# Eight start addresses for the MLP operands of a two-layer decoder trunk, and other cuts at both ends of the program

## The chip, the cores and the metric

One core of a Trainium2 chip runs the whole program. The metric is the device time of one execution in microseconds (us), from the start of the program to its end.

## What is computed

The input has 256 tokens of width 1024 in float32. Two layers are run. Each is an attention with 16 heads of width 64, then an MLP of inner width 4096; after each of the two stands a residual and a layer norm. Cut to what matters:

```python
h = x
for i in range(DEPTH):                       # 2
    ln1_g, ln1_b, w1, w2, ln2_g, ln2_b = channel[i]
    h = layer_norm(DEEPNORM_ALPHA * h + mixers[i % N_MIXERS](h), ln1_g, ln1_b)
    h = layer_norm(DEEPNORM_ALPHA * h + squared_relu_mlp(h, w1, w2), ln2_g, ln2_b)

def squared_relu_mlp(x, w1, w2):
    return jnp.square(jax.nn.relu(x @ w1)) @ w2
```

The mixer of layer 0 is stick-breaking attention, that of layer 1 a softmax attention with rotary positions (with 256 tokens there is one block, so it is plainly causal).

## The kernel before

Every product with a weight matrix is made as three matmuls in the type fp32r: an operand a is split in a high part (ScalarE, a cast) and a low part (VectorE, a minus its high part), and hi\*hi + hi\*lo + lo\*hi is summed in PSUM. The helper `mm3` (line 192) issues the three, `split` (line 201) the cast and the subtraction.

**Weights.** All weight matrices are cut on the host in units of 512x512, 1 MB each. A unit is loaded by SyncE's queue into one of three `raw` buffers and split into `hi` and `lo`, from a pool of five pairs (`Unit`, lines 239 to 263). The first two units are loaded and split in four slices, so that TensorE can begin early; so is the transposed input `xt` (lines 300 to 313).

**Stages of a layer.** The projections of attention run with attention's own work between them (lines 557 to 583), then the output projection `wo` (lines 585 to 611) and the first layer norm, then the MLP in eight chunks c of 512 inner columns each (lines 677 to 701). In chunks 0 and 1 `up_tok` takes x as the stationary operand and streams 512 columns of weights; in chunks 2 to 7 `up` takes weights as stationary and streams 256 columns of x. `down` takes the inner values (`hh`, `hl`) as stationary and streams 512 columns of weights. Per chunk, `up` has 96 matmuls of 256 columns, `up_tok` 48 of 512 columns and `down` 48 of 512 columns. The last two `down` chunks are done token half by token half (t = 0, then t = 1), and each token half is followed by its layer norm (`norm`, line 350) and, in layer 1, by its output (`to_out`, line 388).

**Order.** `Plan` (line 64) sets the order of the instructions on each engine at build time from costs written in the kernel; TensorE's own order is as the code is written, and the other engines' work is drawn in by time and rank.

**Addresses.** Tiles lie one behind another in each partition's memory. `shift(GAP[0])` and `shift(GAP[1])` (lines 217 and 222) put 224 and 288 unused bytes ahead of and behind x, h and v. In the built program the high and low parts of x begin at 96 modulo 128 bytes, those of all weights at 32, those of the inner values (and of attention's output) at 96. Buffers of `t2k` (line 180) are 2080 bytes apart, so the values `r`, which `up_tok` transposes, begin at 0, 32, 64 or 96, by the buffer.

Of the kernel before, what the change touches and what calls it, by code (L numbers as in the profile page):

```python
# [7 lines left out]
F32 = mybir.dt.float32  # L8
# [21 lines left out]
GAP = (224, 288)  # L30
# [124 lines left out]
def trunk(ctx: ExitStack, tc: tile.TileContext, x, xt, cst, cstb, w, ln, out):  # L155
# [12 lines left out]
    small = pool("small", 12)  # L168
# [49 lines left out]
    xh = one.tile([P, KT, T], F32R, tag="xh", name="xh")  # L218
    xl = one.tile([P, KT, T], F32R, tag="xl", name="xl")
# [19 lines left out]
    class Unit:  # L239
        def __init__(self, i):  # L240
# [34 lines left out]
    warm = one.tile([P, 512], BF16, tag="warm", name="warm")  # L275
# [17 lines left out]
    masks = one.tile([P, 2 * DEPTH + 1, P], BF16, tag="masks", name="masks")  # L293
# [56 lines left out]
    def norm(t, banks, ready, gb, after, base):  # L350
        g, b, got = gb
        sm = small.tile([P, 16], F32, tag="sm", name="sm")
        halves = [slice(n * 512, n * 512 + 512) for n in range(2)]
        last = []
        for n, s in enumerate(halves):
            y = dve(512, lambda n=n, s=s: nc.vector.scalar_tensor_tensor(
                h[t][:, s], h[t][:, s], ALPHA, banks[n], op0=ALU.mult, op1=ALU.add),
                after=[ready[n], base], rank=0, give=[("acc", 1)])
            last.append(dve(512, lambda n=n, s=s: nc.vector.bn_stats(sm[:, 6 * n:6 * n + 6], h[t][:, s]), after=[y], rank=0))
        ag = dve(10, lambda: nc.vector.bn_aggr(sm[:, 12:14], sm[:, 0:12]), after=last, rank=0)  # L360
        ep = dve(10, lambda: nc.vector.tensor_scalar(sm[:, 14:15], sm[:, 13:14], LN_EPS, None, op0=ALU.add), after=[ag], rank=0)
# [425 lines left out]
```

## Time and profile before

| | |
|---|---|
| median of 2 runs | 605.96 us (605.09 to 606.82) |
| the profiled execution | 606.12 us |
| its span, first to last instruction | 604.4 us, mean granted TensorE clock 0.993 |
| TensorE matmuls busy | 592.5 us, 98% of the span |
| VectorE, ScalarE busy | 389.5 us (64%), 290.7 us (48%) |
| read from HBM | 107.7 MB, 180 GB/s over the span |

The span lacks 1.7 us of the execution's time. Busy time of TensorE is no pace: matmuls are pipelined, and one shows a duration of some 276 ns (256 columns) though the next starts after about 114 ns. The pace is read from the starts, or from stretches of the chain that hold matmuls alone, by their count.

### The profile page before, as it was taken

The numbers are of one execution on the slowest core, as the hardware profiler recorded it, in microseconds if no ns is written. First come the engines' busy times: TensorE is split into PE (matmuls) and PEld (weight loads), VectorE is DVE, ScalarE is ACT, GpSimd is POOL, SyncE is SP. The second block draws the span as 40 slices with busy tenths as digits, with TensorE's granted clock in tenths as the row PEclk, the third lists the DMA queues.
The fourth block names the chain that finished last, engine by engine and source line by source line (L and its number), as shares of the span: only waits on it lengthen the run. The fifth ranks groups of instructions, "written<-read, shape, count | busy, mean of one in ns | idle before, by whom it ended". The sixth has DMA issues, their size and how long they took to land.

```text
span 604.4 us, 8761 instructions
## 1 busy us (share of the span) xinstructions
PE 592.5 (98%) x3640; PEld 508.3 (84%) x3640; DVE 389.5 (64%) x489; ACT 290.7 (48%) x419; POOL 24.6 (4%) x30
## 2 busy tenths in 40 slices
PE   7999999999999999999999999999999999999994
PEld 6899987878899899898877777778798998898883
DVE  5687774787546445555789777758676537537444
ACT  5676663436435444543535654635356426435410
POOL 0000000000000000000032022001000000000000
PEclk8999999999999999999999999999999999999998
DMA  8984337075565456447165334442764374365201
GB/s 280 367 332 157 110 140 269 21 262 184 201 239 210 154 195 250 157 150 278 65 219 205 140 140 139 140 140 78 270 230 187 140 279 150 153 255 190 90 0 69
DMA packets 17751, 109.31 MB, mean 181 GB/s; under 512 B 1968, under 2 KB 2352, under 8 KB 5680
## 3 DMA queue, kind: packets, MB, share of 16 engines
q1 hardware_dynamic: 17712, 108.76, 48.6%
q8 instruction: 28, 0.46, 0.3%
q14 instruction: 11, 0.09, 0.0%
HBM read 107.71 MB, written 1.05 MB: 180 GB/s over the span
## 4 chain that ended last, share of the span: by engine, by line
PE 95%; DVE 2%; DMA 1%; ACT 1%; SPq 0%; issue 0%; DVEq 0%; ACTq 0%
PE dn_ps L190 29%; PE up_ps L190 28%; PE wo_ps L190 7%; PE qkT_ps L190 7%; PE v_ps L190 7%; PE qk_ps L190 7%; PE sc L190 3%; PE o L502 2%; PE xt L379 1%; DMA raw<-in_wqkv 1%; PE tp L549 1%; DVE lo L205 1%; DVE xl L205 1%; PE ht_ps L656 1%; PE pt_ps L484 1%; PE pt_ps L486 1%
## 5 line engine op out<-in xcount | busy, mean ns | idle before, releaser
L205 DVE TENSOR_TENSOR lo<-raw,hi 128x1024 fp32r<-128x1024 f32 (+1 forms) x196 | 229.7, 1213 | 47.4 <-ACT hi L204 45.7
L204 ACT CAST hi<-raw 128x1024 fp32r<-128x1024 f32 (+1 forms) x196 | 192.0, 1033 | 62.4 <-issue 42.4
L190 PE MATMUL up_ps<-xh,hi 128*128 128x256 f32 x384 | 106.3, 277 | 0.0
L190 PE MATMUL up_ps<-xl,hi 128*128 128x256 f32 x384 | 106.1, 276 | 0.0
L190 PE MATMUL up_ps<-xh,lo 128*128 128x256 f32 x384 | 106.1, 276 | 0.0
L190 PE MATMUL dn_ps<-hi,hl 128*128 128x512 f32 x256 | 100.9, 394 | 0.0
L190 PE MATMUL dn_ps<-lo,hh 128*128 128x512 f32 x256 | 100.4, 392 | 0.0
L190 PE MATMUL dn_ps<-hi,hh 128*128 128x512 f32 x256 | 99.5, 389 | 0.0
L190 PEld LDWEIGHTS up_ps<-xl,hi 128*128 128x128 f32 x384 | 72.1, 188 | 0.5
L190 PEld LDWEIGHTS up_ps<-xh,hi 128*128 128x128 f32 x384 | 72.1, 188 | 0.5
L623 DVE SCALAR_TENSOR_TENSOR r<-up_ps,r 128x512 f32<-128x512 f32 x32 | 22.0, 688 | 77.9 <-ACT r L621 77.9
L190 PEld LDWEIGHTS up_ps<-xh,lo 128*128 128x128 f32 x384 | 72.1, 188 | 0.0
L621 ACT ACTIVATE r<-up_ps 128x512 f32<-128x512 f32 x32 | 19.1, 596 | 94.8 <-PE up_ps L190 94.8
L190 PEld LDWEIGHTS dn_ps<-lo,hh 128*128 128x128 f32 x256 | 48.1, 188 | 10.6
L190 PEld LDWEIGHTS dn_ps<-hi,hh 128*128 128x128 f32 x256 | 48.1, 188 | 10.2
L190 PEld LDWEIGHTS dn_ps<-hi,hl 128*128 128x128 f32 x256 | 48.1, 188 | 9.6
L190 PE MATMUL qkT_ps<-xh,hi 128*128 128x256 f32 x128 | 37.7, 295 | 1.7 <-ACT hi L204 1.7
L190 PE MATMUL qkT_ps<-xh,lo 128*128 128x256 f32 x128 | 36.6, 286 | 0.2 <-DVE lo L205 0.2
L190 PE MATMUL qkT_ps<-xl,hi 128*128 128x256 f32 x128 | 36.3, 284 | 0.0
L204 ACT CAST xh<-xt 128x512 fp32r<-128x512 f32 x12 | 7.0, 587 | 42.9 <-PE xt L379 41.1
L190 PEld LDWEIGHTS qkT_ps<-xh,hi 128*128 128x128 f32 x128 | 24.9, 195 | 2.8 <-ACT hi L204 2.4
L190 PE MATMUL v_ps<-hi,xh 128*128 128x512 f32 x64 | 26.4, 413 | 0.0
(97 smaller groups left out, 888.8 us busy)
## 6 DMA issues: line engine op xcount, KB each, us to landing
raw<-in_w SPq DMA_DIRECT2D x64, 1024.0 KB, 5.0
raw<-in_wqkv SPq DMA_DIRECT2D x22, 1024.0 KB, 5.1
raw<-in_wo SPq DMA_DIRECT2D x8, 1024.0 KB, 4.8
raw<-in_wqkv SPq DMA_DIRECT2D x8, 256.0 KB, 6.1
gb<-in_l_ln_g SPq DMA_DIRECT2D x4, 512.0 KB, 3.6
gb<-in_l_ln_b SPq DMA_DIRECT2D x4, 512.0 KB, 5.0
h<-in_x SPq DMA_DIRECT2D x2, 512.0 KB, 8.1
out<-h SPq DMA_DIRECT2D x4, 256.0 KB, 2.1
```

What stands on the lines that cost most here:

```text
L190: nc.tensor.matmul(ps, sta, mov, start=start, stop=stop)
L204: f = lambda: nc.scalar.copy(hi(), src())
L205: g = lambda: nc.vector.tensor_tensor(lo(), src(), hi().bitcast(F32), op=ALU.subtract)
L379: nc.tensor.transpose(XB[t][:, n, k * P:(k + 1) * P], h[t][:, (4 * n + k) * P:(4 * n + k + 1) * P], ident)
L484: nc.tensor.transpose(ps[:, j, 0:P], pj[:, T:T + P], ident)
L486: nc.tensor.transpose(ps[:, j, T:T + P], pj[:, P:T], ident)
L502: nc.tensor.matmul(o[HD * j:HD * j + HD, 0, kt * P:T], v[kt][:, hd * HD:(hd + 1) * HD], pt[:, 0:T] if kt == 0 else pt[:, T:T + P], start=k ...
L549: nc.tensor.transpose(tb["tp"][:, pr, c0:c0 + P], QK[g, t]["qk"][:, e * T + pr * P:e * T + pr * P + P], ident)
L621: nc.scalar.activation(box["r", n], ps, AF.Relu)
L623: return dve(512, lambda: nc.vector.scalar_tensor_tensor(box["r", n], ps, 0.0, box["r", n], op0=ALU.max, op1=ALU.mult), after=[a], rank=0. ...
L656: nc.tensor.transpose(box["ht"][:, 0, k * P:(k + 1) * P], box["r", 0][:, k * P:(k + 1) * P], ident)
```

## The change

It has three parts.

1. **Places.** Tiles of weight parts and of inner values get 128 bytes more, and the values begin at an offset in them (`apart`, `pair`, `place`). All other operands stay at the places modulo 128 that they have before (weights 32, x 96, inner values and attention's output 96). In the MLPs the places go by chunk c, with PLACE[c] = 32, 0, 16, 48, 64, 80, 96, 112 for c = 0 to 7. Layer 0: both weights of chunk c at PLACE[c], x and inner values at 96. Layer 1: the first weight of chunk c at PLACE[c] and x at 112 (from the first layer norm on); the second weight at 32 and the inner values of chunk c at PLACE[c] + 64 modulo 128, that is 96, 64, 80, 112, 0, 16, 32, 48.
2. **Start.** The slices of x, and those of the first two weight units, are stored on the host one behind another, so that each load reads one contiguous piece; before, each partition's rows of a slice lay 8 KB apart. The tile of zeros for the first matmuls (`warm`) shares its memory with the masks.
3. **End.** In layer 1, for the last token half, the second 512 output columns of the last chunk are made as two halves of 256, each followed by its residual and its statistics; the last scaling and the last output of these columns are cut in halves, too. The statistics' small tiles come from a pool of their own.

```diff
-GAP = (224, 288)
+GAP = (128, 96)
+PLACE = (32, 0, 16, 48, 64, 80, 96, 112)
...
+    xs_hl = [one.tile([P, KT * T + 32], F32R, tag=f"x{s}", name=f"x{s}") for s in "hl"]
+    x_at = [96]
+
+    def xpart(s, k, q):
+        o = x_at[0] // 4
+        return xs_hl[s][:, o:o + KT * T].rearrange("p (k q) -> p k q", k=KT)[:, k, q]
...
+    def apart(pool, n, at, tag, name, k):
+        y = pool.tile([P, n + 32], F32R, tag=tag, name=name)
+        return y[:, at // 4:at // 4 + n].rearrange("p (k q) -> p k q", k=k)
+
+    def place(name, j):
+        if name == "w10" or name == "w20" or name == "w11":
+            return PLACE[j // 2]
+        return 32
+
+    def pair(name, at):
+        return [apart(st, 4 * T, (at + 64) % 128, "s" + s, name + s, 4) for s in "hl"]
...
-                    nc.sync.dma_start(self.raw[:, k0:k1, :], w[name][j][:, k0:k1, :])
+                    nc.sync.dma_start(self.raw[:, k0:k1, :], w["first"][i, k0] if i < 2 else w[name][j])
...
-                            self.hi = splits.tile([P, 4, 512], F32R, tag="hi", name=f"hi{i}")
-                            self.lo = splits.tile([P, 4, 512], F32R, tag="lo", name=f"lo{i}")
+                            self.hi, self.lo = [apart(splits, 2048, place(name, j), s, f"{s}{i}", 4) for s in ("hi", "lo")]
...
-                xs[ks.start // 4][:, ks.start % 4:(ks.stop - 1) % 4 + 1, :], xt[:, ks, :]), rank=3 + 0.01 * (k // 4) + 0.001 * (k % 4) - 0.0005)
+                xs[ks.start // 4][:, ks.start % 4:(ks.stop - 1) % 4 + 1, :], xt[ks.start]), rank=3 + 0.01 * (k // 4) + 0.001 * (k % 4) - 0.0005)
...
+        parts = [(n, c0, c1, tk) for n in range(2) for c0, c1, tk in ready[n]]
+        for i, (n, c0, c1, tk) in enumerate(parts):
+            s = slice(512 * n + c0, 512 * n + c1)
+            y = dve(c1 - c0, lambda n=n, s=s, c0=c0, c1=c1: nc.vector.scalar_tensor_tensor(
+                h[t][:, s], h[t][:, s], ALPHA, banks[n][:, c0:c1], op0=ALU.mult, op1=ALU.add),
+                after=[tk, base], rank=0, give=[("acc", 1)] if c1 == 512 else ())
+            last.append(dve(c1 - c0, lambda i=i, s=s: nc.vector.bn_stats(sm[:, 6 * i:6 * i + 6], h[t][:, s]), after=[y], rank=0))
...
+            fine = [(0, 256), (256, 512)] if len(ready[n]) > 1 else [(0, 512)]
+            for c0, c1 in fine:
+                s = slice(512 * n + c0, 512 * n + c1)
+                end.append(dve(c1 - c0, lambda s=s: nc.vector.scalar_tensor_tensor(
+                    h[t][:, s], h[t][:, s], rs, b[:, s], op0=ALU.mult, op1=ALU.add), after=[pw, cen[n]], rank=0))
+                after(t, n, end[-1], s)
...
+        if l:
+            x_at[0] = 112
...
-                HT[c] = (st.tile([P, 4, T], F32R, tag="sh", name="hh"), st.tile([P, 4, T], F32R, tag="sl", name="hl"))
+                HT[c] = pair("h", (PLACE[c] + 64) % 128 if l else 96)
...
+                loop = [(n, k, c0, c1) for n, c0, c1 in ((0, 0, 512), (1, 0, 256), (1, 256, 512)) for k in range(4)]
...
+        if l == 0:
+            give("first", units[:2].transpose(0, 2, 1, 3))
```

(The pool that `pair` takes from begins at 64 modulo 128, so that the argument of `pair` is the place itself. The places named here are those of the built program.)

Apart from the end, no engine's order changes. On VectorE, the end of the program before (the layer norm of the last token half; `h_91` is its residual stream):

```order
L356 SCALAR_TENSOR_TENSOR h_91<-h_91,dn_ps 128x512
L359 BN_STATS sm<-h_91 128x6
L356 SCALAR_TENSOR_TENSOR h_91<-h_91,dn_ps 128x512
L359 BN_STATS sm<-h_91 128x6
L360 BN_AGGR sm<-sm 128x2
L361 TENSOR_SCALAR sm<-sm 128x1
L363 SCALAR_TENSOR_TENSOR h_91<-h_91,sm,gb_3824 128x512 x2
L367 SCALAR_TENSOR_TENSOR h_91<-h_91,sm,gb_3825 128x512 x2
```

And of the change, the same place (`h_94` is the same tile):

```order
L384 SCALAR_TENSOR_TENSOR h_94<-h_94,dn_ps 128x512
L387 BN_STATS sm<-h_94 128x6
L384 SCALAR_TENSOR_TENSOR h_94<-h_94,dn_ps 128x256
L387 BN_STATS sm<-h_94 128x6
L384 SCALAR_TENSOR_TENSOR h_94<-h_94,dn_ps 128x256
L387 BN_STATS sm<-h_94 128x6
L388 BN_AGGR sm<-sm 128x2
L389 TENSOR_SCALAR sm<-sm 128x1
L392 SCALAR_TENSOR_TENSOR h_94<-h_94,sm,gb_3826 128x512 x2
L399 SCALAR_TENSOR_TENSOR h_94<-h_94,sm,gb_3827 128x512
L399 SCALAR_TENSOR_TENSOR h_94<-h_94,sm,gb_3827 128x256 x2
```

The second pair of residual and statistics became two pairs of half the width, and the last of the two scalings two of half the width; SyncE's last output is cut likewise, and TensorE's last 12 matmuls of 512 columns became 24 of 256.

On SyncE's queue, the first loads before:

```order
L304 DMA h_90<-in_xt 128x256
L248 DMA raw_114<-in_wqkv 128x512
L304 DMA h_90<-in_xt 128x256
L248 DMA raw_114<-in_wqkv 128x512
L304 DMA h_90<-in_xt 128x512
L248 DMA raw_114<-in_wqkv 128x512 x2
L304 DMA h_91<-in_xt 128x512
```

And of the change:

```order
L329 DMA h_93<-in_xt 128x256
L274 DMA raw_116<-in_first 128x512
L329 DMA h_93<-in_xt 128x256
L274 DMA raw_116<-in_first 128x512
L329 DMA h_93<-in_xt 128x512
L274 DMA raw_116<-in_first 128x512 x2
L329 DMA h_94<-in_xt 128x512
```

Order and sizes are the same; the weight slices come from the array `first`, and the slices of x from an array each.

## Rows read from the trace of the kernel before

**Rows 1.** The page: busy time of each engine, share of the span and instructions.
```profile
PE 592.5 (98%) x3640; PEld 508.3 (84%) x3640; DVE 389.5 (64%) x489; ACT 290.7 (48%) x419; POOL 24.6 (4%) x30
```
**Rows 2.** Chain that ended last: start us, us, what, and count of its instructions.
```profile
68.24 3.54 PE qkT_ps L190 x30
75.15 4.10 PE qkT_ps L190 x36
...
167.62 10.91 PE up_ps L190 x96
178.53 10.98 PE dn_ps L190 x48
...
530.84 10.91 PE up_ps L190 x96
541.75 10.98 PE dn_ps L190 x48
```
**Rows 3.** Stretches of one `up` chunk: busy us of each engine, clock, DMA share, GB/s.
```profile
core 0: us, PE busy (x) PEld busy (x) DVE busy (x) ACT busy (x) POOL busy (x), PEclk, DMA share, GB/s
168.50:169.86 1.36, 1.36 (x14) 1.36 (x13) 1.36 (x2) 1.36 (x2) 0.00 (x0) 1.00 0.92 367
177.01:178.37 1.36, 1.36 (x15) 1.36 (x13) 0.00 (x0) 0.00 (x0) 0.00 (x0) 1.00 0.13 48
```
**Rows 4.** Timeline of TensorE in these stretches: start us, duration us, what.
```profile
168.39 0.28 PE L190 MATMUL up_ps<-xh,lo 128*128 128x256 f32 x1
...
169.07 0.28 PE L190 MATMUL up_ps<-xh,lo 128*128 128x256 f32 x1
...
177.12 0.28 PE L190 MATMUL up_ps<-xl,hi 128*128 128x256 f32 x1
...
177.69 0.28 PE L190 MATMUL up_ps<-xh,hi 128*128 128x256 f32 x1
```
**Rows 5.** Chain: the four transposes that follow each of the first `up_tok`.
```profile
132.85 0.44 PE ht_ps L656 x4
...
136.75 0.44 PE ht_ps L656 x4
...
142.01 0.44 PE ht_ps L656 x4
...
147.69 0.44 PE ht_ps L656 x4
```
**Rows 6.** The stretch at the lower clock, and starts of matmuls in it.
```profile
11.80:15.20 3.40, 3.40 (x19) 3.40 (x18) 3.36 (x6) 2.53 (x5) 0.00 (x0) 0.50 1.05 426
...
12.19 0.42 PE L190 MATMUL qkT_ps<-xh,lo 128*128 128x256 f32 x1
...
13.26 0.41 PE L190 MATMUL qkT_ps<-xl,hi 128*128 128x256 f32 x1
```
**Rows 7.** The page: weight loads of `up`; busy us, mean ns of one, idle before.
```profile
L190 PEld LDWEIGHTS up_ps<-xl,hi 128*128 128x128 f32 x384 | 72.1, 188 | 0.5
```
**Rows 8.** The start: TensorE's wait, who ended it, and DMA in two stretches.
```profile
7.80 0.28 PE L190 MATMUL qkT_ps<-xh,lo 128*128 128x256 f32 x1
9.78 0.38 PE L190 MATMUL qkT_ps<-xh,hi 128*128 128x256 f32 x1 [1.71 <-ACT hi L204]
...
8.22 0.71 ACT L309 CAST xh<-h 128x256 fp32r<-128x256 f32 x2 [2.34 <-DMA h<-in_xt]
9.11 1.29 ACT L204 CAST hi<-raw 128x512 fp32r<-128x512 f32 x2 [0.18 <-DMA raw<-in_wqkv]
...
5.00:9.00 4.00, 3.08 (x24) 2.68 (x23) 1.53 (x5) 1.33 (x3) 0.00 (x0) 1.00 0.89 208
9.00:12.70 3.70, 2.69 (x17) 2.49 (x18) 3.36 (x8) 3.37 (x7) 0.00 (x0) 0.87 1.08 416
```
**Rows 9.** Timeline: the end of the program, and an operation of VectorE of half the width.
```profile
596.20 0.40 PE L190 MATMUL dn_ps<-hi,hl 128*128 128x512 f32 x1
596.64 0.69 DVE L356 SCALAR_TENSOR_TENSOR h<-h,dn_ps 128x512 f32<-128x512 f32 x1 [1.33 <-PE dn_ps L190]
597.36 0.69 DVE L359 BATCH_NORM_STATS2 sm<-h 128x6 f32<-128x512 f32 x1
...
599.72 1.41 DVE L367 SCALAR_TENSOR_TENSOR h<-h,sm,gb 128x512 f32<-128x512 f32 x2
...
8.66 0.76 DVE L310 TENSOR_TENSOR xl<-h,xh 128x256 fp32r<-128x256 f32 x2 [2.05 <-ACT xh L309]
```
**Rows 10.** The page: the output's DMA issues, KB each, median us to landing.
```profile
out<-h SPq DMA_DIRECT2D x4, 256.0 KB, 2.1
```

More of the change, by code (lines that the diff above doesn't have):

```diff
@@ L273, in retire @@
         plan.give([("split", n)], clock["pe"])
-    warm = one.tile([P, 512], BF16, tag="warm", name="warm")
+    masks = one.tile([P, 2 * DEPTH + 1, P], BF16, tag="masks", name="masks")
+    warm = masks[:, 0:4, :].rearrange("p a b -> p (a b)")
     nc.gpsimd.memset(warm, 0.0)
@@ L351, in norm @@
         g, b, got = gb
-        sm = small.tile([P, 16], F32, tag="sm", name="sm")
-        halves = [slice(n * 512, n * 512 + 512) for n in range(2)]
+        sm = small.tile([P, 24], F32, tag="sm", name="sm")
+        mv, ve, rs = sm[:, 18:20], sm[:, 20:21], sm[:, 21:22]
         last = []
[L355 to L359, printed above, removed]
@@ L363, in norm @@
+        ag = dve(10, lambda: nc.vector.bn_aggr(mv, sm[:, 0:6 * len(parts)]), after=last, rank=0)
+        ep = dve(10, lambda: nc.vector.tensor_scalar(ve, mv[:, 1:2], LN_EPS, None, op0=ALU.add), after=[ag], rank=0)
+        pw = plan.op("pool", 1.0, lambda: nc.gpsimd.tensor_tensor(rs, ve, nhalf, op=ALU.pow), after=[ep], rank=0)
+        cuts = [slice(n * 512, n * 512 + 512) for n in range(2)]
         cen = [dve(512, lambda s=s: nc.vector.scalar_tensor_tensor(
-            h[t][:, s], h[t][:, s], sm[:, 12:13], g[:, s], op0=ALU.subtract, op1=ALU.mult), after=[ag, got], rank=0) for s in halves]
+            h[t][:, s], h[t][:, s], mv[:, 0:1], g[:, s], op0=ALU.subtract, op1=ALU.mult), after=[ag, got], rank=0) for s in cuts]
@@ L365, in norm @@
         end = []
-        for n, s in enumerate(halves):
-            end.append(dve(512, lambda s=s: nc.vector.scalar_tensor_tensor(
-                h[t][:, s], h[t][:, s], sm[:, 15:16], b[:, s], op0=ALU.mult, op1=ALU.add), after=[pw, cen[n]], rank=0))
-            after(t, n, end[-1])
+        for n in range(2):
+            fine = [(0, 256), (256, 512)] if len(ready[n]) > 1 else [(0, 512)]
[4 more added lines that the diff above has]
+                after(t, n, end[-1], s)
@@ L370, in norm, with to_x @@
         return end
     XB = {}
-    def to_x(t, n, done):
+    def to_x(t, n, done, _):
         def turn():
@@ L386, in trunk, with to_out @@
     XTP = [None] * NT
-    def to_out(t, n, done):
-        s = slice(n * 512, n * 512 + 512)
+    def to_out(t, n, done, s):
         plan.op("sp", 0.75, lambda: nc.sync.dma_start(out[tok(t), s], h[t][:, s]), after=[done], rank=0)
@@ L664, in down @@
             last = c == NFC - 1
-            ready = [None, None]
-            for n, k in [(n, k) for n in range(2) for k in range(4)] if last else [(n, k) for k in range(4) for n in range(2)]:
+            ready = [[], []]
+            if not last:
+                loop = [(n, k, 0, 512) for k in range(4) for n in range(2)]
+            elif l < DEPTH - 1 or t == 0:
+                loop = [(n, k, 0, 512) for n in range(2) for k in range(4)]
+            else:
+                loop = [(n, k, c0, c1) for n, c0, c1 in ((0, 0, 512), (1, 0, 256), (1, 256, 512)) for k in range(4)]
+            for n, k, c0, c1 in loop:
                 plan.wait([us[n].tok[k], HR[c][t][k]])
                 hh, hl = HT[c]
-                mm3(dn[t][n], hh[:, k, tok(t)], hl[:, k, tok(t)], us[n].hi[:, k, :], us[n].lo[:, k, :],
-                    c == 0 and k == 0, last and k == 3)
-                ready[n] = here()
+                mm3(dn[t][n][:, c0:c1], hh[:, k, tok(t)], hl[:, k, tok(t)], us[n].hi[:, k, c0:c1], us[n].lo[:, k, c0:c1],
+                    c == 0 and k == 0, last and k == 3 and c1 == 512)
+                if k == 3:
+                    ready[n].append((c0, c1, here()))
             if t == 1:
@@ L762 @@
     give("x", x)
-    give("xt", x.reshape(T, KT, P).transpose(2, 1, 0))
+    xt = x.reshape(T, KT, P).transpose(2, 1, 0)
+    pieces = {}
+    for k, n in X_LOADS.items():
+        give(f"xt{k}", xt[:, k:k + n, :])
+        pieces[k] = aps[f"xt{k}"]
     cst, cstb = _constants()
```

27 lines of the change are left out of this document (15 added, 12 removed).

## Prediction

> **What bounds the kernel now.** I read the page first: TensorE is busy for 98% of the span, VectorE for 64%, ScalarE for 48% [rows 1]. So the kernel is TensorE's time, and the change can matter in two ways: by the pace at which matmuls follow each other, or by the few microseconds at both ends in which TensorE waits or is done. The busy share says nothing of the pace, so I read the chain of waits next: in the MLPs it is runs of matmuls with nothing between them. An `up` chunk is 96 matmuls of 256 columns in 10.91 us, 113.6 ns each; a `down` chunk is 48 of 512 columns in 10.98 us, 228.8 ns each; in layer 1 the same figures stand [rows 2]. The reader is to see how even that is: the pace is a property of the matmul, not of what runs beside it. It shows again in two stretches of one chunk. In the first, VectorE and ScalarE are busy throughout and DMA moves 367 GB/s; in the second both are idle and DMA moves 48 GB/s [rows 3]. Six matmuls start within 0.68 us (113 ns each) in the one, five within 0.57 us (114 ns) in the other [rows 4].
>
> **The floor.** In the one stretch where the clock is at 0.50, the level of 1.2 GHz, matmuls of 256 columns start 1.07 us apart by five, 214 ns each [rows 6]: 256 columns at 1.2 GHz are 213.3 ns, so nothing is lost there. At 2.4 GHz the same would be 106.7 ns, and 213.3 ns for 512 columns. The MLPs lose 7 ns of each 256-column matmul and 15.5 ns of each 512-column one. That loss is all that better places could win.
>
> **Places.** 1152 matmuls of 256 columns (6 chunks x 96 x 2 layers) and 816 of 512 columns get a new place for an operand (`up_tok` 48 + 96, `down` 7 chunks x 48 in each layer; chunk 0 keeps its places apart from x in layer 1). They take 1152 x 0.1136 + 816 x 0.2288 = 131 + 187 = 318 us, 53% of the span. No row shows these matmuls at other places, so I bound the cost from both sides.
> - Lowest: the whole loss goes, 1152 x 7.0 ns + 816 x 15.5 ns = 8.1 + 12.6 = 20.7 us.
> - Highest that a row of the same matmul shows: in layer 0's attention, runs of the same form are either at 114 ns (36 in 4.10 us) or at 118 ns (30 in 3.54 us), both at the places 32 and 96 [rows 2]. If all 1152 fell to 118 ns, they would cost 1152 x 4.4 = 5.1 us. That two levels stand at one pair of places also says that place alone does not set the pace.
> - Nearest row for the place itself: the transposes after `up_tok` read `r` from buffers that begin at 0, 96, 64 and 32 modulo 128, in this order, with the other operand always at 32. Four take 0.44 us each time [rows 5]. They move a column only every 0.86 ns, so they could hide a small stall; but they are the only matmuls here whose places differ.
>
> I take zero, since it is what that nearest row shows, and since memory traffic of other engines leaves the pace alone [rows 3, 4]. The casts, subtractions and DMAs that write to the new places lie on engines with slack [rows 1]; should one grow by a tenth, VectorE would still be below 72%.
>
> The Trainium skill ("SBUF — State Buffer", section on the two separate sides) says that TensorE has ports of its own and never waits on anyone, with a second, independent read port for weight loads. By that rule the places change nothing at all, and the sum is that of the two ends alone; the equal pace beside busy and idle engines [rows 3, 4] agrees as far as other engines go, while no run here shows the two read ports against each other.
>
> **Start.** TensorE waits from about 7.9 us (0.11 us after its start at 7.80) to 9.78, 1.9 us. The wait's chain: the cast of the first weight unit's third slice starts at 9.11 when its DMA lands, and the slice of x ahead of it had landed only at 8.2 [rows 8]. From 5 to 9 us the DMA moves 208 GB/s, after 9 us 416 GB/s [rows 8]. Contiguous slices could speed up the first stretch. If they took the wait away, the stretch at the lower clock that follows it would go, too: about 16 matmuls at 214 instead of 114 ns, 1.6 us [rows 6]. The most is 1.9 + 1.6 = 3.5 us. Against it: after 9 us the queue still carries slices with the same 8 KB stride (x and the second unit), at full speed [rows 8]. So the stride is not plainly the cause, and I count a quarter, 0.9 us; the bounds are 0 and 3.5. What is saved is kept: TensorE is the bound behind it. The masks' DMA now has to wait for the warm matmuls, which are over 5 us before it is issued.
>
> **End.** After the last matmul (start 596.20) residual and statistics take 0.69 us each on VectorE [rows 9]. At 256 columns an operation of VectorE takes 0.38 us (0.76 for two) [rows 9], so the two save 2 x 0.31 = 0.6 us; the first half's pair lies beside the second half's matmuls (12 x 113.6 = 1.36 us for 0.76 us of work). The 24 matmuls of 256 columns take 24 x 113.6 = 2.73 us in place of 12 x 228.8 = 2.75 us. Cutting the last scaling adds one operation's fixed cost: 0.70 + 2 x 0.38 against 1.41 us, +0.05. The last output is 128 KB in place of 256; of its 2.1 us [rows 10] I take off 0.25 us, half of what 256 KB take at some 400 GB/s, with 0 as the other bound. Together -0.8 us (-0.5 to -1.0).
>
> **Sum.** The profiled execution took 606.12 us, 1.7 us more than its span, and 0.2 us more than the median of 605.96. 606.12 - 0.9 - 0.8 + 0 = 604.4 us. Two per cent, 12.1 us, is about what a measurement of this kernel can tell from no change.
>
> **Rivals.**
> 1. *The places move the loss* (faster). With half of the 20.7 us gone the time is 594.1 us, with all of it 583.8. For: the loss is there at 2.4 GHz and not at 1.2 [rows 2, 6], so something that reads memory cannot quite follow, and 16 bytes might matter to it. Against: the places go through all eight, so a good one serves an eighth of the chunks, and the new ones would have to be nearly all better. By over 2% only if more than half of the loss goes.
> 2. *Operands at one place collide* (slower). The next weights are loaded while the present columns stream; a load takes 188 ns [rows 7] and hides only because loads overlap matmuls and each other. If both reads met when their operands begin at the same place, the load would come out of hiding and a 256-column matmul would last 188 instead of 113.6 ns, +74 ns; at 512 columns it stays covered by 228.8. Equal places stand in layer 0's chunk 6 (96 and 96) and layer 1's chunk 7 (112 and 112): 192 matmuls of 256 columns, 14.3 us, 618.7 us. It is slower than 2% from 186 such matmuls on (13.8 us above 604.4); with 288 more at 16 bytes' distance it would be 640 us. For: before, all pairs are 64 apart, the farthest there is, so no row tells what nearness costs. Against: rows 5, where 32 met 32 at no cost.
> 3. *The slow level* (within 2%). Matmuls of 256 columns fall to 118 ns: 604.4 + 5.1 = 609.5 us at most.
> 4. *The change does nothing at either end*: DMA stays at 208 GB/s, and the end saves 0.5: 605.6 us.
>
> The Trainium skill ("TensorE: Matmul & The Clock Gate", on the 56 ns gap) gives N / 2.4 GHz plus about 2.5 ns for back-to-back bf16 matmuls. By that figure the first rival would have 4.4 ns and 13 ns to win, some 15.7 us, and end no lower than 588.7 us; no run here shows a matmul at that pace.
>
> **Chances.** The forecast, with rival 4 as its edge: 0.56. Slow level: 0.10. Rival 1: 0.12, of which 0.08 over 2%. Rival 2: 0.18, and 0.04 for slow places of another pattern, all over 2%. That makes 0.08 faster, 0.56 + 0.10 + 0.04 = 0.70 within 2%, 0.22 slower. The range from 596 to 624 us holds the forecast, the slow level, the smaller gains of rival 1 and the equal places of rival 2; it leaves out the larger gains and nearness beyond equal places, about 0.17. The forecast's own range is 601.5 to 606.5.
>
> **What would show it.** In the chain, `up` chunks of 10.9 us and `down` chunks of 11.0 us in both layers at every c: places are neutral. Chunks that differ from their neighbours by c show the opposite, and by how much at which place; rival 2 would show only in chunk 6 of layer 0 and chunk 7 of layer 1. At the start, a DMA rate well over 208 GB/s from 5 to 9 us, TensorE's wait below 1 us, and no stretch at the lower clock would show the contiguous loads at work. At the end, 0.38 us operations and a last output that lands sooner. The prediction is wrong if any chunk's pace is off by more than 4%.

## The result, and the profile of the changed kernel

The changed kernel takes 614.38 us (median of 2 runs, 613.8 to 614.96), against 605.96 before: a ratio of 1.0144, 95% interval 1.0115 to 1.0172. It is slower by 8.4 us; the forecast was 604.4. Its profiled span is 613.1 us against 604.4, the mean granted clock 0.996 against 0.993. VectorE and ScalarE are as busy as before; TensorE is busy 9 us longer (the counterpart of [rows 1], page of the changed kernel):

```profile
PE 601.6 (98%) x3652; PEld 513.5 (84%) x3652; DVE 389.6 (64%) x492; ACT 290.4 (47%) x419; POOL 24.6 (4%) x30
```

**The heavy stages.** The chain that ended last, of the changed kernel (start us, us, what, count), answers to [rows 2]:

```profile
74.87 4.34 PE qkT_ps L192 x36
...
100.54 12.79 PE wo_ps L192 x54
...
157.52 11.17 PE dn_ps L192 x48
168.69 11.32 PE up_ps L192 x96
...
236.09 11.31 PE up_ps L192 x96
247.40 11.09 PE dn_ps L192 x48
258.48 11.32 PE up_ps L192 x96
...
459.61 11.17 PE dn_ps L192 x48
...
560.30 11.28 PE up_ps L192 x96
```

Every `up` chunk takes 11.23 to 11.32 us where it took 10.91 (96 matmuls: 117 to 118 ns each against 113.6), every `down` chunk 11.01 to 11.20 where it took 10.98. Three things are to be seen. First, it is nearly the same for all chunks: the chunks whose operands begin at one place, 236.09 (layer 0, c = 6) and 560.30 (layer 1, c = 7), are no slower than 258.48 beside them. Second, stages whose places were not touched are slower, too: layer 0's attention (36 matmuls in 4.34 us, where the 36 of [rows 2] took 4.10), the output projection (100.54, 12.79 us; before, 12.58) and both `down` chunks of c = 0 (157.52 and 459.61), which keep 32 and 96. Third, it is not the granted clock, which is 0.996 over the span. The line of the output projection before is:

```profile
100.49 12.58 PE wo_ps L190 x54
```

So no wait has been added in these stages: a matmul of the three-part products takes some 1 to 7 ns longer on average (0.03 us over 48 in the mildest `down` chunk, 0.24 us over 36 in layer 0's attention).

**The start.** Busy time, clock and DMA in the two stretches of [rows 8], and TensorE's longest wait there, both of the changed kernel:

```profile
5.00:9.00 4.00, 3.53 (x24) 2.83 (x22) 2.04 (x5) 1.35 (x4) 0.00 (x0) 1.00 0.96 289
9.00:12.70 3.70, 2.94 (x23) 2.61 (x22) 3.19 (x7) 3.56 (x8) 0.00 (x0) 1.00 1.06 412
```
```profile
9.66 0.39 PE L192 MATMUL qkT_ps<-xh,hi 128*128 128x256 f32 x1 [0.53 <-ACT hi L206]
```

DMA moves 289 GB/s in the first stretch where it moved 208, TensorE waits for 0.53 us where it waited for 1.71, and the clock, which had fallen to 0.87 in the second stretch and 0.50 behind it, stays at 1.00.

**The end.** From the end of the last matmul (604.97) to the end of the span are 8.1 us, against 7.8 before (last matmul over at 596.60, span 604.4). The cut end is not shorter but longer; why is told with the experiments.

### The profile page after: what moved, and what is told of

It is laid out like the page before. It is cut to its first block, busy times and chain, and to the rows that moved or that the text cites. A ratio compares the mean times of both kernels' runs of the same rounds, so it can differ in the third digit from the quotient of the medians.

```text
span 613.1 us, 8790 instructions
## 1 busy us (share of the span) xinstructions
PE 601.6 (98%) x3652; PEld 513.5 (84%) x3652; DVE 389.6 (64%) x492; ACT 290.4 (47%) x419; POOL 24.6 (4%) x30
## 4 chain that ended last, share of the span: by engine, by line
PE 95%; DVE 2%; DMA 1%; ACT 1%; SPq 0%; issue 0%; DVEq 0%; ACTq 0%
PE dn_ps L192 29%; PE up_ps L192 28%; PE wo_ps L192 7%; PE v_ps L192 7%; PE qkT_ps L192 7%; PE qk_ps L192 7%; PE sc L192 3%; PE o L533 2%; PE xt L411 1%; DMA raw<-in_first 1%; PE tp L580 1%; DVE lo L207 1%; DVE xl L207 1%; PE ht_ps L689 1%; PE pt_ps L515 1%; PE pt_ps L517 1%
## 5 line engine op out<-in xcount | busy, mean ns | idle before, releaser
L192 PE MATMUL up_ps<-xh,hi 128*128 128x256 f32 x384 | 107.7, 280 | 0.0
L192 PE MATMUL up_ps<-xl,hi 128*128 128x256 f32 x384 | 107.7, 280 | 0.0
L192 PE MATMUL up_ps<-xh,lo 128*128 128x256 f32 x384 | 107.5, 280 | 0.0
L192 PE MATMUL dn_ps<-hi,hh 128*128 128x512 f32 (+1 forms) x260 | 101.9, 392 | 0.0
L192 PE MATMUL dn_ps<-hi,hl 128*128 128x512 f32 (+1 forms) x260 | 101.4, 390 | 0.0
L192 PE MATMUL dn_ps<-lo,hh 128*128 128x512 f32 (+1 forms) x260 | 101.2, 389 | 0.0
L192 PE MATMUL qk_ps<-hi,xh 128*128 128x512 f32 x64 | 26.5, 415 | 0.0
```

What stands on the lines that cost most here:

```text
L192: nc.tensor.matmul(ps, sta, mov, start=start, stop=stop)
```

## Experiments

All kernels are the changed one with the edits shown. The expectations name theories by letters: **P**, the places modulo 128 cost time; **B**, the 128 bytes added to each tile cost it, since they move operands beyond modulo 128; **S**, something at the start sets a state that lasts; **J**, what costs is a jump of the address modulo 256 from one matmul to the next; **R**, what costs is the distance modulo 256 between the moving and the stationary operand; **L**, a slow level, once entered, stays; **T** and **E** are on the end. Addresses modulo 256 in this part are read from the built programs.

Why B could be at all: before, a part of a weight is 8192 bytes per partition and x high and x low lie 8192 apart, so all high parts, low parts and buffers of one kind begin at one address modulo 256. With 128 bytes more per tile, the next tile begins 128 bytes further modulo 256. All places modulo 128 are as the change states them; modulo 256, high and low parts and successive buffers alternate.

| kernel | median us | ratio to before, 95% | `up` chunk us | `down` chunk us |
|---|---|---|---|---|
| before | 605.96 | 1 | 10.91 | 10.98 to 10.99 |
| changed | 614.38 | 1.0144 (1.0115 to 1.0172) | 11.23 to 11.32 | 11.01 to 11.20 |
| e1_one_place | 617.48 | 1.0187 (1.0172 to 1.0203) | 11.31 to 11.62 | 11.13 to 11.20 |
| e2_no_pad | 604.1 | 0.9968 (0.9956 to 0.998) | 10.91 | 10.98 to 10.99 |
| e3_pad_w | 607.9 | 1.0039 (1.0027 to 1.0051) | 10.90 to 11.41 | 11.05 to 11.10 |
| e4_pad_x | 610.23 | 1.0068 (1.0053 to 1.0083) | 11.31 | 10.99 |
| e6_pad_x256 | 604.48 | 0.9969 (0.9955 to 0.9983) | 10.91 | 10.98 to 10.99 |
| e7_pad_h | 606.95 | 1.0017 (1.0005 to 1.0029) | 10.89 to 10.90 | 11.13 to 11.20 |
| e5_lo_apart | 610.41 | 1.0068 (1.0045 to 1.0091) | 10.90 to 11.40 | 10.98 to 11.20 |
| e8_pad_w_even | 610.11 | 1.0063 (1.004 to 1.0086) | 10.89 to 11.31 | 11.00 to 11.20 |
| e9_places_even | 613.33 | 1.0122 (1.0075 to 1.017) | 11.20 to 11.52 | 10.90 to 11.34 |
| e10_one_chunk | 606.45 | 1.0017 (1.0006 to 1.0029) | 10.89 to 11.40 | 10.98 to 11.20 |
| e11_old_end | 603.99 | 0.9971 (0.996 to 0.9982) | 10.91 | 10.98 to 10.99 |
| e12_own_bank | 603.08 | 0.9955 (0.9942 to 0.9968) | 10.91 | 10.98 to 10.99 |

The last two columns are from the chain of each kernel's trace (chunks with 96 `up` and 48 `down` matmuls in one piece). A ratio is to runs of the kernel before that were taken together with the kernel (their medians are 605.33 to 606.32 us), so it is not quite the quotient of two medians of the table.

### Is it the places, or the larger tiles?

**e1_one_place**: all chunks at one place again, tiles still larger.

```diff
-PLACE = (32, 0, 16, 48, 64, 80, 96, 112)
+PLACE = (32,) * 8
...
-            x_at[0] = 112
+            x_at[0] = 96
```

> The change with every place put back (weights 32, x and inner values 96 modulo 128 in all chunks), its larger tiles and both cut ends kept. If the places modulo 128 cost the 8 us (theory P), this takes 603 to 606 us, with `up` chunks at 10.9 and `down` chunks at 11.0 us. If it is the 128 bytes between tiles that were added for them, which put the buffers at unequal addresses beyond 128 (theory B), it stays at 612 to 615 us with `up` at 11.3 us.

**e2_no_pad**: no larger tiles and no places; of the change only start and end are left. All operands of the three-part products are where they were before, modulo 512; the masks, and constants that transposes read, are not.

```diff
-GAP = (128, 96)
+GAP = (224, 288)
+PADX, PADW, PADH = (0, 0, 0)
...
-    xs_hl = [one.tile([P, KT * T + 32], F32R, tag=f"x{s}", name=f"x{s}") for s in "hl"]
+    xs_hl = [one.tile([P, KT * T + PADX // 4], F32R, tag=f"x{s}", name=f"x{s}") for s in "hl"]
...
-        y = pool.tile([P, n + 32], F32R, tag=tag, name=name)
-        return y[:, at // 4:at // 4 + n].rearrange("p (k q) -> p k q", k=k)
+        y = pool.tile([P, n + (PADW if pool is splits else PADH) // 4], F32R, tag=tag, name=name)
+        return y[:, :n].rearrange("p (k q) -> p k q", k=k)
```

> The change without the larger tiles and without new places: every buffer where the kernel before has it modulo 512, only the cuts at the start and the end. Theories P and B: 603 to 606 us, `up` chunks at 10.9 us. If the cut start sets another lasting state of TensorE (theory S), 610 us or more, with `up` chunks at 11.3 us.

The places are gone in e1 and it is the slowest of all, 1.0187 (its 617.48 us lie even above the range expected for B); the larger tiles are gone in e2 and it is faster than before, 0.9968, with every chunk at its old pace. So B holds: the larger tiles cost 2.19% (e1 less e2), 13.3 us of 606, give or take some 1.2. The eight places give about 0.43% of it back (the changed kernel less e1), 2.6 us, though by the two intervals it can be 0.6 to 4.6 us; the two ends give 0.32%, 1.9 us. P falls as the cause of the loss, and S with it, since e2 has the changed start.

### Which tiles, and by what step?

From e2, one kind of tile at a time is made larger: the ten weight buffers (**e3_pad_w**, PADW = 128), the two x tiles (**e4_pad_x**, PADX = 128), the inner values and attention's output (**e7_pad_h**, PADH = 128); and the x tiles by twice as much (**e6_pad_x256**, PADX = 256). The edit of e3:

```diff
-PADX, PADW, PADH = (0, 0, 0)
+PADX, PADW, PADH = (0, 128, 0)
```

> As the kernel without larger tiles, but 128 bytes more in each of the ten weight buffers, which all still begin at 32 modulo 128. Theory P: 603 to 606 us. Theory B, if weight buffers among each other matter: 609 to 615 us, slow in `up` and `down` alike.

> As the kernel without larger tiles, but 128 bytes more in each of the two tiles of x, so that the low part of x begins 8320 bytes behind the high part in place of 8192. Theory P: 603 to 606 us. Theory B, if any two operands at unequal addresses beyond 128 cost: `up` chunks at 11.3 us and `down` chunks at 11.0 us, 606 to 611 us in all.

> The kernel without larger tiles, but 128 bytes more in each of the six buffers of inner values and attention's output, which are stationary operands. Theory J: `down` chunks go from 10.98 to some 11.08 us, since the stationary operand jumps by 128 modulo 256 between high and low part; `up` keeps 10.9 us; 605.5 to 607 us in all. If only jumps of moving operands cost: 604 us.

> As the kernel with 128 bytes more in the tiles of x, but 256 more: the low part of x lies 8448 bytes behind the high part. If addresses count modulo 256, 603 to 605.5 us and `up` chunks at 10.9 us; if they count modulo 512 or more, 609 to 611 us and 11.3 us as with 128 bytes.

Chain of e4_pad_x, where x low begins 8320 bytes behind x high:

```profile
118.71 6.18 PE up_ps L193 x27
...
155.30 10.99 PE dn_ps L193 x48
166.28 11.31 PE up_ps L193 x96
177.59 10.99 PE dn_ps L193 x48
188.58 11.31 PE up_ps L193 x96
```

Chain of e6_pad_x256, where it begins 8448 bytes behind:

```profile
154.55 10.98 PE dn_ps L193 x48
165.53 10.91 PE up_ps L193 x96
```

Chain of e7_pad_h:

```profile
165.34 10.90 PE up_ps L193 x96
176.24 11.20 PE dn_ps L193 x48
```

In e4 the `up` chunks, which stream x, are slow by 0.40 us each, 4.2 ns per matmul; `down`, which does not read x, keeps 10.99. Not all that reads x is slow: `up_tok`, where x is the stationary operand (118.71, 27 matmuls), takes the 6.18 us that it takes before. In e7 `up` keeps its pace and `down`, which has the inner values as stationary operand, takes up to 11.20. In e6 both are at the old pace, and its time is that of e2 (0.9969 against 0.9968). So for x a distance of 128 bytes costs and one of 256 costs nothing: its address counts modulo 256.

The three kinds cost, against e2, 0.71%, 1.00% and 0.49%, together 2.20%, close to the 2.19% of all three at once. The intervals leave some 0.4% open, and stage by stage the sum does not hold: over the ten `down` chunks of the chain the mean is 0.09 us above e2 in e3 and 0.19 in e7, but in e1 it is 0.18 and not 0.28. So the three are the whole loss as far as the times tell, but their costs are not independent. Neither range expected for e3 holds its 607.90 us, which lies between the two.

### What about an address makes a matmul slow?

**e5_lo_apart**: the low parts of the MLPs' weights begin D bytes further, D by chunk; all else as in e2, apart from low-part tiles that are 256 bytes larger (`apart` is called with these values for low parts and with 0 for high parts).

```diff
+APART = ((0, 128, 0, 32, 64, 96, 128, 192), (64, 192, 16, 48, 80, 112, 160, 224))
...
-        y = pool.tile([P, n + 32], F32R, tag=tag, name=name)
+        y = pool.tile([P, n + (64 if tag == "lo" else 0)], F32R, tag=tag, name=name)
...
+        return APART[int(name[2])][j // 2] if name[:2] in ("w1", "w2") else 0
```

> The kernel without larger tiles, but the low parts of the MLP weights begin D bytes behind the residue of the high parts modulo 256, D by chunk: layer 0 0, 128, 0, 32, 64, 96, 128, 192; layer 1 64, 192, 16, 48, 80, 112, 160, 224. Theory J (what costs is a jump of an operand's address modulo 256 from one matmul to the next): chunk 2 of layer 0 (D = 0) keeps 10.9 us for `up` and 11.0 us for `down`, chunk 6 (D = 128) takes 11.05 and 11.08 us as with padded weights, the others lie at or between these; 605 to 608 us in all. If the jump counts by more than 256, chunk 2 of layer 0 is slow as well. Theory P (places modulo 128): chunks with D = 128 are as fast as that with D = 0.

**e8_pad_w_even**: as e3, and 128 bytes between the pools of high and low parts, so that the two parts of a unit agree modulo 256 and only successive units differ by 128. The 128 bytes also move the inner values and attention's output, from 96 to 224 modulo 256.

```diff
+    between = pool("between", 1)
+    splitl = pool("splitl", LIVE)
...
+    between.tile([P, 32], F32, tag="between", name="between")
...
-                            self.hi, self.lo = [apart(splits, 2048, place(name, j), s, f"{s}{i}", 4) for s in ("hi", "lo")]
+                            self.hi, self.lo = [apart(sp, 2048, 0, s, f"{s}{i}", 4) for s, sp in (("hi", splits), ("lo", splitl))]
```

> As the kernel with 128 bytes more in each weight buffer, but with 128 more bytes between the high and the low parts, so that the two parts of a unit agree modulo 256 and only different units differ. Theory J: `up` chunks back at 10.9 us, `down` between 10.98 and 11.08 us (its two units alternate), 604 to 606 us. If it is the distance of moving to stationary operand modulo 256 that counts (theory R), as slow as with padded weights: `up` 11.05 us, 607 to 608.5 us.

**e9_places_even**: the eight places for the MLPs' weights (layer 1: 128 more), but tiles 256 bytes larger, so that all buffers of a chunk agree modulo 256; x at 224, inner values at 192 and attention's weights at 32 throughout.

```diff
-GAP = (128, 96)
+GAP = (96, 0)
+PADX, PADW, PADH = (0, 256, 0)
...
-        if name == "w10" or name == "w20" or name == "w11":
-            return PLACE[j // 2]
+        if name[:2] in ("w1", "w2"):
+            return PLACE[j // 2] + 128 * int(name[2])
```

> What the change set out to do, without its side effect: MLP weights begin at PLACE[c] in layer 0 and at PLACE[c] + 128 in layer 1 (16 places modulo 256), but all weight buffers lie 8448 bytes apart, so that high and low parts and all units at one place agree modulo 256; x and inner values stay 64 away from the place 32. If agreement modulo 256 from one matmul to the next is all that counts (theory J), every chunk is at 10.9 and 11.0 us and the total is 603 to 606 us. If the distance of moving to stationary operand modulo 256 counts (theory R), chunk 0 of layer 0 keeps 11.0 us for `down` and the others differ by their place, 604 to 612 us.

**e10_one_chunk**: as e5, but the low parts of two chunks alone are moved, chunk 3 of layer 0 by 32 bytes and chunk 4 of layer 1 by 64.

```diff
-APART = ((0, 128, 0, 32, 64, 96, 128, 192), (64, 192, 16, 48, 80, 112, 160, 224))
+APART = ((0, 0, 0, 32, 0, 0, 0, 0), (0, 0, 0, 0, 64, 0, 0, 0))
```

> Low parts 32 bytes off in chunk 3 of layer 0 alone, and 64 bytes off in chunk 4 of layer 1 alone; every other address agrees modulo 256 with the kernel before. If addresses alone set the pace, only `up` and `down` of these two chunks are slow (about 0.5 and 0.1 to 0.2 us each), 604.5 to 606 us. If a level once entered stays (theory L), chunks behind them at unchanged addresses are slow as well, at 11.3 and 11.2 us, until something sets them back: 606 to 612 us.

Chain of e10_one_chunk in layer 0. In this order stand `up` 3, `down` 1, `up` 4, `down` 2, `up` 5, `down` 3, `up` 6, `down` 4, `up` 7; only the first and `down` 3 (220.12) read moved weights:

```profile
164.73 11.40 PE up_ps L193 x96
176.13 11.20 PE dn_ps L193 x48
187.33 10.90 PE up_ps L193 x96
198.23 10.98 PE dn_ps L193 x48
209.22 10.91 PE up_ps L193 x96
220.12 11.09 PE dn_ps L193 x48
231.21 11.31 PE up_ps L193 x96
242.52 11.20 PE dn_ps L193 x48
253.72 10.90 PE up_ps L193 x96
```

The moved chunks are slow, as J and R both say. What neither says: `down` 1 behind the first one (176.13, 11.20), and `up` 6 and `down` 4 behind the second (231.21, 11.31 and 242.52, 11.20), are slow, too, though none of their operands was moved; then the old pace is back. In layer 1 it is the same behind the moved `up` 4 (`down` 2 takes 11.20 us), but not behind the moved `down` 4 (11.14), where `up` 7 takes 10.89. It is no clock. Stretches within `up` 3, the unmoved `down` 1, and the recovered `up` 4 (columns as in [rows 3]; the clock is the third number from the end):

```profile
165.00:176.00 11.00, 11.00 (x95) 11.00 (x94) 4.63 (x4) 3.02 (x4) 0.00 (x0) 1.00 0.68 262
176.30:187.00 10.70, 10.70 (x48) 8.66 (x47) 7.22 (x8) 6.21 (x9) 0.00 (x0) 1.00 0.31 116
187.50:198.00 10.50, 10.50 (x95) 10.50 (x94) 4.63 (x4) 3.12 (x4) 0.00 (x0) 1.00 0.68 266
```

The clock is 1.00 in all three, and the stretches of the slow `up` 3 and the fast `up` 4 have the same load beside them. So a slow pace can be carried on by matmuls that would not enter it, for a stage or two, and L holds in this weaker form; it does not stay for good. Nor does every slow stage hand its pace on: in e4 each `down` behind a slow `up` keeps 10.99, and in e7 each `up` behind a slow `down` takes 10.89 to 10.90. From e10 alone a rival would remain: its low-part tiles are 256 bytes larger, so that in the slow unmoved stages the low parts of the two units lie 256 apart modulo 512. The next chain shows the handing on without it.

Chain of e5_lo_apart in layer 0: `up` chunks with D = 64, 96, 128 and 192, in this order, and, behind the first of them (at 198.82), `down` 2, whose D is 0:

```profile
187.46 11.36 PE up_ps L193 x96
198.82 11.20 PE dn_ps L193 x48
210.01 11.32 PE up_ps L193 x96
...
232.42 10.90 PE up_ps L193 x96
...
254.46 11.30 PE up_ps L193 x96
```

In e5 and in e10, `down` 2 of layer 0 reads all operands of its 48 matmuls at the very same addresses. It takes 11.20 us in e5, behind a moved `up` 4 (11.36), and 10.98 in e10 (198.23), behind an unmoved one (10.90). What differs is the stage ahead, and with it the places to which VectorE writes later low parts meanwhile; for `down` 1 of e10 those are unmoved (five pairs of buffers do not reach to the next moved ones), and it is slow all the same. The expectation of e5 had 11.0 us for this chunk, or a slow one if jumps count by more than 256; e10 has the same addresses and is fast, so that is not the reason. The 610.41 us of e5 lie above the expected 605 to 608.

Of the four `up` chunks, the one with D = 128 is at the old pace, the others are slow. Yet in e4 128 bytes between the two parts of x, the moving operand, made `up` slow. So one rule on the distance of high and low part does not cover both.

Chain of e9_places_even, layer 1: `up` 3, `up` 5, `down` 3, `up` 6, `down` 4:

```profile
468.90 11.20 PE up_ps L193 x96
...
513.65 11.51 PE up_ps L193 x96
525.16 11.34 PE dn_ps L193 x48
536.51 11.51 PE up_ps L193 x96
548.02 10.90 PE dn_ps L193 x48
```

Here no operand jumps modulo 256 within a chunk, so J expected the old pace throughout; all `up` chunks are slow, by 0.29 to 0.61 us. J alone falls. What is not excluded is a jump from one stage to the next whose pace is then kept, as in e10, since in e9 each stage begins at another place. The place counts, in both directions: `down` 4, whose weights and inner values both begin at 192 modulo 256, takes 10.90 us, less than any before; `down` 3, weights at 176, takes 11.34; `up` 6, x and weights both at 224, is at 11.51 no faster than `up` 5 at 224 and 208. So equal places neither collide nor help in general. The 613.33 us lie above both expected ranges. R's forecast of 11.0 us for `down` 0 of layer 0 (it took 11.20) was not tested: weights at 32 and inner values at 192 are not as far apart modulo 256 as 160 and 96 are before.

e8 closes the list. Three `up` chunks of its layer 0:

```profile
166.59 11.31 PE up_ps L195 x96
...
233.96 10.90 PE up_ps L195 x96
...
255.91 10.90 PE up_ps L195 x96
```

With high and low parts in step, `up` chunks lie at 10.89 to 10.90 or at 11.30 to 11.31 and nowhere between. The four of ten at 10.89 to 10.90 are those where the last product of the `down` ahead and the first of the `up` itself both read weights at 160 modulo 256; in the six others one of them or both read at 32. The chunks at 166.59 and 255.91 both read x at 96 and all weights at 160, as before the change; one is slow and one is fast, and the stage ahead differs. The chunk at 233.96 keeps the fast pace through its second half, whose weights are at 32. So in these chunks the pace is set at their beginning, and kept. The time of e8 (1.0063) is above that of e3 (1.0039), where the parts were out of step, and above both expected ranges; the inner values moved as well, so the two kernels do not compare the step between the parts alone.

### The two ends

In e2 the first `down` chunk of layer 0 starts at 154.44 us where it started at 156.64 before: the start is worth 2.2 us there. But the whole gain of e2's span is 1.8 us (602.6 against 604.4), so the end gives some back. Timeline of VectorE at the end of e2_no_pad, with the last row of TensorE behind it:

```profile
592.49 0.69 DVE L388 BATCH_NORM_STATS2 sm<-h 128x6 f32<-128x512 f32 x1
594.49 0.42 DVE L385 SCALAR_TENSOR_TENSOR h<-h,dn_ps 128x256 f32<-128x256 f32 x1 [1.30 <-PE dn_ps L193]
594.95 0.43 DVE L388 BATCH_NORM_STATS2 sm<-h 128x6 f32<-128x256 f32 x1
595.29 0.40 DVE L385 SCALAR_TENSOR_TENSOR h<-h,dn_ps 128x256 f32<-128x256 f32 x1
595.73 0.43 DVE L388 BATCH_NORM_STATS2 sm<-h 128x6 f32<-128x256 f32 x1
```
```profile
594.17 0.28 PE L193 MATMUL dn_ps<-hi,hl 128*128 128x256 f32 x1
```

The residual of the first half does not start when its own 12 matmuls are over, some 1.3 us earlier; VectorE idles for 1.30 us and starts at 594.49, when the very last matmul is done. Both halves lie in one PSUM bank. In the built program the first half's operation waits for a count that TensorE raises only with its last matmul, the second half's for nothing: one wait, made by the program, covers the whole bank. What a read beside the matmuls would do was not tried. Then four operations of half the width stand behind the last matmul in place of two whole ones.

**e11_old_end**: e2 with the end of the kernel before, so the start alone. **e12_own_bank**: e2 with the last 12 matmuls in a bank of their own, and their sum added by one more operation of 256 columns; the residual ahead of it covers all 512 columns. The edit of e11:

```diff
-            elif l < DEPTH - 1 or t == 0:
-                loop = [(n, k, 0, 512) for n in range(2) for k in range(4)]
             else:
-                loop = [(n, k, c0, c1) for n, c0, c1 in ((0, 0, 512), (1, 0, 256), (1, 256, 512)) for k in range(4)]
+                loop = [(n, k, 0, 512) for n in range(2) for k in range(4)]
```

And of e12:

```diff
+                own = c0 == 256
+                if own and k == 0:
+                    plan.wait(take=[("acc", 1)])
+                    dn[t].append(abank("dn_ps"))
+                to = dn[t][2][:, :256] if own else dn[t][n][:, c0:c1]
...
+            if c0 == 256:
+                y = dve(256, lambda s=s: nc.vector.scalar_tensor_tensor(
+                    h[t][:, s], h[t][:, s], 1.0, banks[2][:, :256], op0=ALU.mult, op1=ALU.add),
+                    after=[tk, y], rank=0, give=[("acc", 1)])
```

> This is e2_no_pad with the end as in the kernel before (the last matmuls 512 columns wide, one residual and one statistics per bank, scalings and outputs uncut); of the change only the start is left. Theory T (the cut end wins nothing, since the residual of its first half waits for the last matmul: both halves write one PSUM bank, and VectorE's operation waits for the last write to it; it costs 8.1 us from the last matmul to the end of the span in e2_no_pad, 7.8 in the kernel before): 7.8 us from the last matmul on, span 602.3, time 603.8, ratio to before about 0.9965, and the whole gain is that of the start, 2.1 us. Theory E (the cut end is worth its 0.8 us, as predicted, and the tail of e2_no_pad is noise): 8.9 us from the last matmul on, span 603.4.

> This is e2_no_pad with the last 12 matmuls (columns 256 to 511 of the last bank, last chunk) in a PSUM bank of their own; the residual and statistics ahead of them can then run beside these matmuls, and their sum is added by one more operation of 256 columns. Theory T: the first of the operations starts at once when its own 12 matmuls are over, some 1.3 us ahead of the last matmul; behind the last matmul only two operations of 0.43 us stand in place of four; the tail falls from 8.1 to 7.3 us, span 601.8, time 603.3, ratio to before about 0.9955. If the operation waits for the last matmul whatever bank it reads, the tail stays at 8.1 us or more, span 602.6 to 602.9.

Timeline of VectorE at the end of e12_own_bank:

```profile
592.40 0.69 DVE L391 SCALAR_TENSOR_TENSOR h<-h,dn_ps 128x512 f32<-128x512 f32 x1
593.13 0.43 DVE L394 BATCH_NORM_STATS2 sm<-h 128x6 f32<-128x256 f32 x1
593.77 0.42 DVE L386 SCALAR_TENSOR_TENSOR h<-h,dn_ps 128x256 f32<-128x256 f32 x1 [0.21 <-PE dn_ps L193]
594.22 0.43 DVE L394 BATCH_NORM_STATS2 sm<-h 128x6 f32<-128x256 f32 x1
```

The first two now run beside the last matmuls (the last is over at 593.73), and two operations are left behind it. From the last matmul to the end of the span: 7.8 us before and in e11 (593.80 to 601.6), 8.1 in e2, 7.4 in e12 (593.73 to 601.1). T holds and E falls: the cut end costs 0.3 us as made, and wins 0.4 with a bank of its own. That the median of e12 is 0.9 us below that of e11 is within their intervals, so the 0.4 us rests on the traces. In both, the first `down` starts at 153.7 us, so over three executions, and against the one trace of the kernel before, the start is worth 2.2 to 3.0 us there. By the medians e11, the start alone, gains 0.29%, 1.8 us (1.1 to 2.4). The two edits of the start, contiguous slices and the shared tile, were not run apart. e12, with the start, the end in two banks, and every operand of the three-part products at its old address modulo 256, is the fastest kernel here: 603.08 us, 0.45% below before.

## Why the prediction was wrong

The time lies inside the range, but by luck: it lies beyond the slow level's 609.5 us, in the part that was kept for equal places, and those cost nothing. The forecast was a gain of 1.7 us, and it became a loss of 8.4. Step by step:

- **What bounds the kernel** was right: all that was lost or won shows in TensorE's pace and at the two ends.
- **The floor** was a fair bound: 227.1 ns per 512-column matmul (e9, `down` 4) is the best seen, 228.8 before. Of a loss of 15.5 ns, 1.7 were to be had at one of the places tried.
- **Places, taken as zero: the step that failed**, in three ways. The added 128 bytes were not counted at all; I looked at addresses modulo 128, where they vanish, and no row told me that 128 is the right modulus (it is 256, e4 against e6). They cost 13.3 us. Second, I counted only the MLPs' matmuls with a new place, 1968 of them; the larger tiles moved operands of attention as well, whose products slowed, too (`wo`: 54 matmuls by 0.21 us, 3.9 ns each). Third, the "nearest row", the transposes, misled: they move a column only every 0.86 ns, as the prediction itself said, and what they showed did not hold for the three-part products (why they show no cost was not tested). The places as such are not free either: in e9 no operand jumps within a chunk, and it still lies 1.5% above e2. The prediction's own sign, a chunk off by more than 4%, never showed (11.32 against 10.91 us is 3.8%): many small losses made up the 8.4 us.
- **Rival 3, the slow level, was the right mechanism**: the prediction read both levels, 114 and 118 ns at one pair of places, from [rows 2], and the changed kernel runs at the slow one nearly throughout. Its price of "5.1 us at most" held for 1152 matmuls of 256 columns (they did cost about 11.31 less 10.91 us per chunk, 12 chunks, 4.8 us). What was missed is that matmuls of 512 columns have such a second level, too, at which `down` takes 11.20 in place of 10.98. And "place alone does not set the pace" was read as a reason for zero; it was a sign that addresses and what ran before set it together, as e5 and e10 show. The 30 matmuls of [rows 2] that took 3.54 us take 3.42 us in e2, e11 and e12, with its operands at the same addresses modulo 512.
- **Rival 2, equal places collide**, falls: its two chunks are as fast as their neighbours (236.09 and 560.30), and in e9 equal places gave the fastest `down` of all. Had it held, 14.3 us would have shown in two chunks; what happened was 0.3 to 0.4 us in each `up` chunk and 0.03 to 0.2 in each `down` chunk.
- **Start, -0.9**: right in kind, too small: -1.8 by the median of e11, -2.2 to -3.0 by the traces. The chain was read rightly (wait, then the lower clock behind it); quartering the bound because other strided slices ran at full speed was the error. With contiguous slices DMA moves 280 to 328 GB/s in that stretch in e2, e11 and e12.
- **End, -0.8**: nothing gained: +0.3 by the tails of the traces, no difference by the medians of e2 and e11 (0.9968 and 0.9971). The failed step is "the first half's pair lies beside the second half's matmuls". A 256-column operation also took 0.40 to 0.43 us, not 0.38, and the smaller last output saved under 0.1 us, not 0.25 (from the last scaling's end to the end of the span, 3.2 us in e2 and 3.3 before). Half of what 256 KB take at 400 GB/s is 0.32 us besides; the sum hardly changes by it.
- The errors of the ends cancel (e2: -1.9 us by its ratio, predicted -1.7), so the miss of 10 us is that of the places: 13.3 less 2.6, 10.7 us, with some 1 us of uncertainty on the first and 2 us on the second.

The Trainium skill ("SBUF — State Buffer", on the two separate sides) says that TensorE never waits on anyone and that weight loads have a second, independent read port. The equal pace beside busy and idle engines [rows 3, 4] agrees as far as other engines go; but e4 against e6, two kernels that differ in 128 bytes of one tile's address, shows 11.31 against 10.91 us for the same 96 matmuls, which a rule without addresses leaves out. Here the measurement decides. The chances had 0.04 for "slow places of another pattern", all of it over 2%, and nothing for such a loss within 2%, which is what came.

The Trainium skill ("PSUM — Partial Sum Buffer", on bank collisions) says that two engines must not use one bank at the same time. By it the two halves must not overlap in one bank. In e2 they did not, by the program's own wait (1.30 us idle), and with a bank of their own in e12 they did; no run here shows the two engines in one bank at once.

## What to carry to other kernels

When a change makes tiles larger or shifts pools, list the address of every TensorE operand before and after, modulo a power of two well above the step moved, and count each product whose operands got another distance from each other; "the same place modulo 128" is not "the same place". If a trace already shows one form of matmul at two paces, price the slow one for every matmul of the kernel, not for the edited stage alone. And before splitting a reduction at the end so that its first half runs early, ask which buffer its wait is on: two halves of one PSUM bank were released together.

## What the runs showed of the hardware

- The pace of three-part fp32r matmuls depends on the addresses of their operands, at a granted clock of 1.00; 128 bytes between the two parts of x cost, 256 do not (e4, e6). There are two main levels: 10.91 and 11.31 us for 96 of 256 columns, 10.98 and 11.20 for 48 of 512. Per matmul that is 0.40 us / 96 = 4.2 ns and 0.22 us / 48 = 4.6 ns: about the same for both widths, so it looks like a fixed time per matmul rather than a slower stream. Other mixes lie between or beyond: e9 also showed 10.90 and 11.34 for `down`, and `up` took up to 11.52 in e9 and 11.62 in e1.
- For `down`, with parts in step, the distance from inner values to weights goes with the level: at 64 modulo 256 it takes 10.98 to 11.00 us (160 and 96 in e2, 32 and 224 in e8, 0 and 192 in e9), at 192 it takes 11.19 to 11.20 (160 and 224 in e8, 128 and 192 in e9). Behind a moved stage it takes 11.20 at 64, too (e5, e10).
- The slow level can be handed on: stages whose operands had not moved ran at it behind one that had moved (e10), for one or two stages, and then recovered; at the very same addresses `down` 2 took 11.20 us in e5 and 10.98 in e10. Not every slow stage does it (e4, e7).
- With contiguous slices the DMA rate of the first loads (5 to 9 us) was 280 to 354 GB/s in the thirteen kernels that have them, 208 before, and the clock stayed at 1.00 in the changed kernel where it had fallen to 0.50 after a wait of 1.71 us.

**What stays open.** Why the step is 4 to 5 ns per matmul, which pair of accesses meets, and what ends a slow stretch. Jumps between successive matmuls (J) and the distance of moving and stationary operand (R) each explain part: e9 rules out J alone, and `down` 2 in e5 and e10 rules out any rule on the present operands alone. That the level is handed on was seen, its carrier was not.
